# Backward scan outputs in token order, one set of turning products instead of two

## The chip, the cores and the metric

The kernel runs on one core of a Trainium2 chip. The metric is the device time of one execution in microseconds (us). In the text PE is TensorE (matrix products), DVE is VectorE, ACT is ScalarE, POOL is GpSimd and SP is SyncE, whose queue issues most DMAs. "L1300" is line 1300 of the kernel as it stands in the profile before.

## The reference, cut to what matters

One layer of a hybrid backbone runs over 640 tokens (512 latent, 128 context): a normalisation, a projection `w_in`, then 16 heads of a two-directional delta-rule scan beside a chunked gMLP, a projection `w_out`, and a SwiGLU mixer. The part that the change touches is the end of the scan:

```python
for d in range(2):                       # 0: forward, 1: backward
    ...
    y, s_fin = _delta_scan(rh, decay, kd, vh, -kk, kk * heads(a), s0[:, d], reverse=(d == 1))
    out = out + _group_norm(y, lp['gn_w'], lp['gn_b']) \
        + jnp.sum(rh * kd * lp['r_k'], axis=-1, keepdims=True) * vh
o = out.reshape(B, T, D_A) * gate
```

So the scan outputs `y` of both directions are normalised for each token and head, and summed for each token.

## The kernel before

All matrices with channels on partitions are 128 channels by 640 tokens. A "pair" p (0 to 7) is two heads, 128 channels. The scan is done in chunks of 64 tokens, ten chunks (eight of latent tokens, two of context).

**First stage** (to about 1085 us). For each pair and direction d, `rows` builds the tile `R`: for each chunk a half `R[:, :, 0, :]` made of the removal keys and a half `R[:, :, 1, :]` made of the queries `zr`. The function `rev` turns the tokens of each chunk round for d = 1, so that in the backward direction both halves lie in the order of the scan. `chunks` multiplies `X` (keys) with `R`, which gives for each chunk a 128 x 128 block; its right half, query against key, is masked (a query sees keys up to itself) into the tile `GR` and stored in DRAM with other pieces as the record of the chunk, `d_S`.

**Scan stage** (about 1085 to 1368 us). Time advances in "hops". `recur(p)` is a generator that takes three hops for each of eight steps; a new pair starts every 13 hops (`OFF`), and takes 26, so two pairs run side by side. In a step, the state products `w_ps` (L1193) are added on DVE to the tile `W` (L1202), which `u_ps` (L1213) multiplies; its result is copied into the record `rec` by DVE (L1217) and then ACT (L1218); `s_ps` (L1240) makes the new state from the record, and DVE turns it into `SN` (L1248) with the help of `SG` (L1224). `y_ps` (L1166, L1176) makes the outputs of the 64 tokens, which ACT copies into `u.Y[:, d, chunk, :]` (L1181), tokens on partitions (heads on two halves of them).

When a pair's scan has ended, `norm(p)` runs over the next hops: POOL subtracts the mean from `u.Y` (L1277), ACT squares, DVE sums, POOL takes the power -0.5 (L143) and multiplies (L1287). Two hops later `join(p, 0)` and one hop after it `join(p, 1)` turn five chunks each back to channels: in `join` (L1300), each product takes a 64 x 64 block of `u.Y` as weights and streams a 64 x 64 matrix past it, `I2` (the unit matrix) for d = 0 and `J2` (the unit matrix with its columns reversed) for d = 1. Both products add up in the same place of PSUM, so the sum over directions and the turn round of d = 1 are done by PE. DVE then joins the bonus term (L1303, `bv`). In the two hops after that `gate(p, hf)` makes four products `pmm` (L1312), and DVE multiplies `bv` by them (L1313).

Between these pieces PE is filled with products of `w_out` from the job list `m3` (L1081 to L1083, `big`), and with transposes of the input (L1338, `pxT`). The left operand of these is loaded by SP (`o_load`, L1067, `ol<-d_o`), rounded by ACT (L1068, `oh`) and split on DVE (L1069, `ol`).

What sets the order: on PE the scan stage is written out by hand (`manual_schedule`), so PE executes it in the order in which the code emits it. On the other engines, and in SP's queue, a scheduler orders the instructions by its own estimate of times; each engine then executes strictly in that order.

Of the kernel before, what the change touches and what calls it, by code (L numbers as in the profile page):

```python
# [10 lines left out]
F32 = mybir.dt.float32  # L11
# [3 lines left out]
ALU = mybir.AluOpType  # L15
# [4 lines left out]
P = 128  # L20
# [5 lines left out]
CH = 64  # L26
# [63 lines left out]
def flow_step(ctx: ExitStack, tc, x_prompt, x_sample, state_rwkv, c, c_ctx, w_mod, b_mod,  # L90
# [4 lines left out]
    V, S, G, TE = nc.vector, nc.scalar, nc.gpsimd, nc.tensor  # L95
# [21 lines left out]
    cb = cbx.enter_context(tpool(name="constb", bufs=1))  # L117
# [4 lines left out]
    I2 = cb.tile([P, CH], F32, name="I2")  # L122
    for h in range(2):
        s = slice(CH * h, CH * h + CH)
        V.tensor_copy(I2[s, :], ident[s, s])
    J2 = cb.tile([P, CH], F32, name="J2")
    V.tensor_copy(J2, I2[:, ::-1])
    mask = cb.tile([P, P], F32, name="mask")
    ones16 = cb.tile([P, CH], BF16, name="ones16")
    V.memset(ones16, 1.0)  # L130
# [237 lines left out]
    v3 = lambda ap: ap.rearrange("p (c t) -> p c t", t=CH)  # L368
# [195 lines left out]
    def take_k(pr, p):  # L564
        o = pairs[p]
        o.GB, o.dd = {}, {}
        zr, zv = o.zr, o.zv
# [63 lines left out]
        def rows(d, inner):  # L631

            rev = (lambda ap: ap[:, :, ::-1]) if d else (lambda ap: ap)
            tha, g3, i3 = thas[d], v3(gams[d]), v3(Ls[d])
            Rs[d] = R = bz.tile([P, NCH, 2, CH], F32, tag="R", name="R")
            ra = rev(R[:, :, 0, :])
            if d:
                V.tensor_mul(ra[:, :, 0:CH - 1], n3[:, :, 0:CH - 1], g3[:, :, 1:CH])
                S.copy(ra[:, :, CH - 1], n3[:, :, CH - 1])
            else:  # L640
                V.tensor_mul(ra[:, :, 1:CH], n3[:, :, 1:CH], g3[:, :, 0:CH - 1])
                S.copy(ra[:, :, 0], n3[:, :, 0])
            yield 0.8
            V.tensor_mul(rev(R[:, :, 1, :]), v3(zr), g3)
            yield 0.8
            nc.sync.dma_start(d_S[p, :, d, :, F_R:F_R + P], R.rearrange("p c s t -> p c (s t)"))
            Zs[d] = Z = bz.tile([P, NCH, 2, CH], F32, tag="Z", name="Z")
            vsrc = d_vt[p, d].rearrange("(c t) v -> t c v", t=CH)
            for h in range(2):
                nc.sync.dma_start(Z[hsl(h), :, h, :], vsrc[:, :, hsl(h)])  # L650
            f = fs if d == 0 else bk.tile([P, T], F32, tag="t1", name="f", bufs=2)
            V.tensor_scalar(f, tha, kah[:, p:p + 1], ka1[:, p:p + 1], op0=ALU.mult, op1=ALU.add)
            V.tensor_mul(f, f, zk)
            yield 1.2
            V.scalar_tensor_tensor(out=tha, in0=tha, scalar=1.0, in1=nkk, op0=ALU.add, op1=ALU.mult)
            yield 0.8

            for e in ((0, 1), (1, 0)):
                V.scalar_tensor_tensor(out=rev(X[hsl(e[0]), :, e[1], :]), in0=v3(tha)[hsl(e[0])], scalar=-0.5,
                                       in1=i3[hsl(e[0])], op0=ALU.mult, op1=ALU.mult)  # L660
            yield 1.5
            if d == 1:
                V.tensor_add(fs, fs, f)
            yield from inner
            V.tensor_mul(rev(X[0:64, :, 0, :]), v3(f)[0:64], i3[0:64])
            V.tensor_mul(rev(X[64:128, :, 1, :]), v3(f)[64:128], i3[64:128])
            yield 1.5

        def chunks(d):

            R, Z = Rs[d], Zs[d]
            n = 2 * p + d
            mixM.until(lambda: len(merged) > n - 4)
            o.GB[d] = GB = bp.tile([P, NCH, CH], F32, tag=f"GB{n % 4}", name="GB")

            GA = bk.tile([P, NCH, CH], F32, tag="GA", name="GA")
            for (c0, c1) in ((0, 4), (4, 8), (8, NCH)):
                two = [ps.rearrange("p (c t) -> p c t", t=P) for ps in both("pG")]
                in_turn([lambda cc=cc, h=h: TE.matmul(
                    two[h][:, cc - c0, :], X[hsl(h), cc].rearrange("p s t -> p (s t)"),  # L680
                    R[hsl(h), cc].rearrange("p s t -> p (s t)"), start=True, stop=True)
                    for cc in range(c0, c1) for h in range(2)])
                S.copy(GB[osl(0), c0:c1, :], two[0][osl(0), 0:c1 - c0, 0:CH])
                for h in (1, 0):
                    s, q, ps = hsl(h), osl(h), two[h]
                    mb = mask.unsqueeze(1).to_broadcast([P, c1 - c0, P])
                    GR = bk.tile([P, 4, CH], F32, tag="GR", name="GR", bufs=2)
                    V.tensor_tensor(out=GR[:, 0:c1 - c0, :], in0=ps[:, 0:c1 - c0, CH:P], in1=mb[:, :, CH:P], op=ALU.mult)
                    V.tensor_tensor(out=GA[s, c0:c1, :], in0=ps[s, 0:c1 - c0, 0:CH], in1=mb[s, :, 0:CH], op=ALU.mult)
                    if h:  # L690
                        S.copy(GB[q, c0:c1, :], ps[q, 0:c1 - c0, 0:CH])
                    nc.sync.dma_start(d_S[p, :, d, c0:c1, F_G + CH * h:F_G + CH * h + CH], GR[:, 0:c1 - c0, :])
                yield 0.5 * (c1 - c0)

            for (c0, c1) in ((0, 8), (8, NCH)):
                two = [ps.rearrange("p (c t) -> p c t", t=CH) for ps in both("pXT")]
                in_turn([lambda cc=cc, h=h: TE.transpose(
                    two[h][:, cc - c0, :], X[hsl(h), cc].rearrange("p s t -> p (s t)"), ident[hsl(h), hsl(h)])
                    for cc in range(c0, c1) for h in range(2)])
                for h in range(2):  # L700
                    ps = two[h]
                    XT = bz.tile([P, 8, CH], F32, tag="XT", name="XT", bufs=2)
                    S.copy(XT[:, 0:c1 - c0, :], ps[:, 0:c1 - c0, :])
                    nc.sync.dma_start(d_S[p, :, d, c0:c1, F_X + CH * h:F_X + CH * h + CH], XT[:, 0:c1 - c0, :])
                yield 0.2 * (c1 - c0)
            two = [ps.rearrange("p (c t) -> p c t", t=CH) for ps in both("pW0")]
            for c0 in (0, 5):
                ps = two[c0 // 5][:, 0:5, :]
                for cc in range(c0, c0 + 5):
                    for h in range(2):  # L710
                        TE.matmul(ps[osl(h), cc - c0, :], GA[hsl(h), cc, :], Z[hsl(h), cc, h, :], start=True, stop=True)
                for h in range(2):
                    S.copy(Z[osl(h), c0:c0 + 5, h, :], ps[osl(h)])
                yield 1.0
            nc.sync.dma_start(d_S[p, :, d, :, F_Z:F_Z + P], Z.rearrange("p c h v -> p c (h v)"))
            o.dd[d] = db.tile([8, NCH, 16, 16], F32, tag=f"dd{d}", name="dd")
            for gq in range(8):
                q = gq % 4
                BQ.dma_start(o.dd[d][gq].rearrange("c s t -> s c t"),
                             GB[16 * gq:16 * gq + 16, :, 16 * q:16 * q + 16])  # L720
# [376 lines left out]
    with ExitStack() as ph:  # L1097
# [160 lines left out]
        def norm(p):  # L1258
# [14 lines left out]
            for d in range(2):  # L1273
                y, ys = u.Y[:, d], u.ys[:, d]
                G.tensor_scalar(ys, ys, 1.0 / CH, None, op0=ALU.mult)
                for (a, b) in HV:
                    G.tensor_tensor(out=y[:, a:b], in0=y[:, a:b], in1=bc(ys[:, a:b], b - a), op=ALU.subtract)  # L1277
                yield
                sq = rw.tile([P, NCH, CH], F32, tag="sq", name="sq")
                for (a, b) in HV:  # L1280
                    S.activation(sq[:, a:b], y[:, a:b], AF.Square)
                    V.tensor_reduce(out=ys[:, a:b], in_=sq[:, a:b], axis=AX.X, op=ALU.add)
                yield
                G.tensor_scalar(ys, ys, 1.0 / CH, GN_EPS, op0=ALU.mult, op1=ALU.add)
                rsqrt(ys, ys)
                for (a, b) in HV:
                    G.tensor_tensor(out=y[:, a:b], in0=y[:, a:b], in1=bc(ys[:, a:b], b - a), op=ALU.mult)  # L1287
                yield

        HV = ((0, 5), (5, NCH))  # L1290

        def join(p, i):

            u = U[p]
            a, b = HV[i]
            ps = po.tile([P, 5, CH], F32, tag="g", name="pO")
            for cc in range(a, b):
                for h in range(2):
                    for d in range(2):
                        TE.matmul(ps[hsl(h), cc - a, :], u.Y[hsl(h), d, cc, :], (J2 if d else I2)[hsl(h), :],  # L1300
                                  start=(d == 0), stop=(d == 1))
            dst = v3(u.bv)[:, a:b, :]
            V.scalar_tensor_tensor(out=dst, in0=ps, scalar=prm[:, C_GW + p:C_GW + p + 1],  # L1303
                                   in1=dst, op0=ALU.mult, op1=ALU.add)
# [866 lines left out]
```

## Time and profile before

| | |
|---|---|
| median of 3 runs | 3190.33 us (3187.9 to 3195.78) |
| the profiled execution | 3191.31 us, of which its span is 3189.5 us |
| granted PE clock | 0.991 |
| PE busy | 3075.3 us, 96% of the span |
| DVE busy | 2347.6 us, 74% |
| ACT busy | 1474.9 us, 46% |
| POOL busy | 1220.2 us, 38% |

The profiled execution is 1.0 us above the median. "Busy" of PE counts a product until its modelled end, so short products that are issued one behind the other overlap in it.

### The profile page before, as it was taken

The numbers are of one execution on the slowest core, as the hardware profiler recorded it, in microseconds if no ns is written. First come the engines' busy times: TensorE is split into PE (matmuls) and PEld (weight loads), VectorE is DVE, ScalarE is ACT, GpSimd is POOL, SyncE is SP. The second block draws the span as 40 slices with busy tenths as digits, with TensorE's granted clock in tenths as the row PEclk, the third lists the DMA queues.
The fourth block names the chain that finished last, engine by engine and source line by source line (L and its number), as shares of the span: only waits on it lengthen the run. The fifth ranks groups of instructions, "written<-read, shape, count | busy, mean of one in ns | idle before, by whom it ended". The sixth has DMA issues, their size and how long they took to land.

```text
span 3189.5 us, 72242 instructions
## 1 busy us (share of the span) xinstructions
PE 3075.3 (96%) x28216; PEld 2861.3 (90%) x28216; DVE 2347.6 (74%) x4120; ACT 1474.9 (46%) x3216; POOL 1220.2 (38%) x1065
## 2 busy tenths in 40 slices
PE   6899999999999999999999999999999999999997
PEld 4688878788878888899999999999999999999997
DVE  4566777667775678767877878777777788877788
ACT  3344544454444444346544444444444445444365
POOL 2001121221122024411465666656655655555542
PEclk9999999999999999999999999999999999999999
DMA  9767786777777688475344434443344365553453
GB/s 370 245 192 202 217 231 172 212 199 212 221 202 193 214 275 268 153 210 162 97 125 128 122 107 127 119 121 119 109 130 126 108 194 156 163 160 119 143 165 123
DMA packets 740439, 550.89 MB, mean 173 GB/s; under 512 B 141056, under 2 KB 673504, under 8 KB 731264
## 3 DMA queue, kind: packets, MB, share of 16 engines
q1 hardware_dynamic: 727136, 532.47, 55.3%
q0 software_dynamic: 10624, 13.23, 1.8%
q8 instruction: 222, 3.64, 0.5%
q14 instruction: 121, 0.99, 0.1%
q10 hardware_dynamic: 2336, 0.57, 0.1%
HBM read 437.79 MB, written 110.95 MB: 172 GB/s over the span
## 4 chain that ended last, share of the span: by engine, by line
PE 73%; DVE 10%; issue 6%; DMA 6%; ACT 3%; POOL 2%; SPq 0%; DVEq 0%; POOLq 0%; ACTq 0%
PE P L1688 15%; PE P L1685 15%; PE P L1686 15%; PE big L196 5%; PE big L200 4%; PE big L197 4%; DMA raw<-in_w_in_dram 1%; PE pm L948 1%; DVE lo L1466 1%; PE big L1081 1%; PE big L1524 1%; PE big L1525 1%; PE big L1526 1%; PE big L1082 1%; PE big L1083 1%
## 5 line engine op out<-in xcount | busy, mean ns | idle before, releaser
L1685 PE MATMUL P<-xo,hi 128*128 128x320 f32 x2352 | 700.5, 310 | 0.2 <-ACT hi L1465 0.2
L1686 PE MATMUL P<-xo,hi 128*128 128x320 f32 x2352 | 700.4, 309 | 0.0
L1466 DVE TENSOR_TENSOR lo<-raw,hi 128x512 fp32r<-128x512 f32 x526 | 517.8, 989 | 161.6 <-ACT hi L1465 158.7
L1465 ACT CAST hi<-raw 128x512 fp32r<-128x512 f32 x526 | 326.7, 622 | 468.4 <-PE P L1686 397.6
L1688 PE MATMUL P<-xo,lo 128*128 128x320 f32 x2352 | 441.8, 310 | 4.1 <-DVE lo L1466 4.1
L196 PE MATMUL big<-h_hi,hi 128*128 128x320 f32 x1376 | 438.2, 325 | 7.8 <-ACT hi L174 4.4
L1685 PEld LDWEIGHTS P<-xo,hi 128*128 128x128 f32 x2352 | 442.3, 188 | 0.5 <-ACT hi L1465 0.5
L1686 PEld LDWEIGHTS P<-xo,hi 128*128 128x128 f32 x2352 | 442.7, 188 | 0.0
L197 PE MATMUL big<-h_lo,hi 128*128 128x320 f32 x1376 | 422.6, 314 | 0.8 <-DVE h_lo L360 0.8
L1594 POOL TENSOR_TENSOR raw<-raw 128x512 f32<-128x512 f32 x252 | 410.5, 1638 | 10.1 <-DVE lo L1466 1.8
L1688 PEld LDWEIGHTS P<-xo,lo 128*128 128x128 f32 x2352 | 370.0, 188 | 4.9 <-DVE lo L1466 4.9
L1685 PE MATMUL P<-xd,hi 128*128 128x320 f32 x1232 | 367.8, 310 | 6.1 <-ACT P L2079 2.8
L1686 PE MATMUL P<-xd,hi 128*128 128x320 f32 x1232 | 366.8, 309 | 0.0
L200 PE MATMUL big<-h_hi,lo 128*128 128x320 f32 x1376 | 319.8, 312 | 3.9 <-DVE lo L175 2.1
L196 PEld LDWEIGHTS big<-h_hi,hi 128*128 128x128 f32 x1376 | 261.8, 190 | 58.2 <-issue 26.1
L175 DVE TENSOR_TENSOR lo<-raw,hi 128x512 fp32r<-128x512 f32 x268 | 185.4, 695 | 157.6 <-ACT hi L174 153.9
L1594 POOL TENSOR_TENSOR t<-raw 128x512 f32<-128x512 f32 x84 | 123.7, 1472 | 427.5 <-DMA raw<-in_w_ffn_up_dram 415.9
L1465 ACT CAST hi<-rawd 128x512 fp32r<-128x512 f32 (+1 forms) x288 | 167.1, 586 | 225.3 <-PE P L1686 148.9
L174 ACT CAST hi<-raw 128x512 fp32r<-128x512 f32 x268 | 164.4, 617 | 225.9 <-PE big L197 84.9
L197 PEld LDWEIGHTS big<-h_lo,hi 128*128 128x128 f32 x1376 | 261.6, 190 | 5.8 <-DVE h_lo L360 1.9
L1466 DVE TENSOR_TENSOR lo<-rawd,hi 128x512 fp32r<-128x512 f32 (+1 forms) x288 | 231.9, 812 | 24.9 <-ACT hi L1465 24.2
L1688 PE MATMUL P<-xd,lo 128*128 128x320 f32 x1232 | 236.6, 310 | 4.2 <-DVE lo L1466 4.2
(408 smaller groups left out, 6129.7 us busy)
## 6 DMA issues: line engine op xcount, KB each, us to landing
wt<-in_w_mod_dram SPq DMA_DIRECT2D x96, 1024.0 KB
raw<-in_w_ffn_gate_dram SPq DMA_DIRECT2D x182, 256.0 KB
raw<-in_w_ffn_up_dram SPq DMA_DIRECT2D x182, 256.0 KB
rec<-d_S SPq DMA_DIRECT2D x80, 576.0 KB
raw<-in_w_in_dram SPq DMA_DIRECT2D x172, 256.0 KB
rawd<-in_w_ffn_down_dram SPq DMA_DIRECT2D x128, 256.0 KB
raw<-in_w_out_dram SPq DMA_DIRECT2D x96, 256.0 KB
xd<-d_os SPq DMA_DIRECT2D x66, 320.0 KB
```

Of the source, the lines that this page charges most:

```text
L174: S.copy(hi, raw)
L175: V.tensor_sub(lo, raw, hi.bitcast(F32))
L196: TE.matmul(halves[hf], hi[:, k, :], h_hi[:, kb, s], start=(kb == 0), stop=False)
L197: TE.matmul(halves[hf], hi[:, k, :], h_lo[:, kb, s], start=False, stop=False)
L200: TE.matmul(halves[hf], lo[:, j - 4 * q, :], h_hi[:, j, s], start=False, stop=(j == KB - 1))
L948: TE.matmul(pm[32 * j:32 * j + 2, :], cT[:, 2 * (kb + u):2 * (kb + u) + 2], quad[:, u, j, :], start=(kb + u == 0), stop=(kb + u == KB - 1) ...
L1465: S.copy(hi[:, 0:nk], raw[:, 0:nk])
L1466: V.tensor_sub(lo[:, 0:nk], raw[:, 0:nk], hi[:, 0:nk].bitcast(F32))
L1594: G.tensor_tensor(out=o[:, 0:nk], in0=p[:, 0:nk], in1=q[:, 0:nk], op=ALU.subtract)
L1685: TE.matmul(ps, hi[:, k, :], xk[:, 0, :], start=q == 0 and k == 0 and not filled, stop=False)
L1686: TE.matmul(ps, hi[:, k, :], xk[:, 1, :], start=False, stop=False)
L1688: TE.matmul(ps, lo[:, k, :], x(i, 4 * q + k)[:, 0, :], start=False, stop=q == nq - 1 and k == nk - 1 and last)
```

## The change

The queries of the backward direction are stored in the natural order of tokens instead of the order of the scan. The order of queries in `R` is the order of the scan's output rows, so the outputs of d = 1 come out in natural order too, and the mask of their scores is read with its columns reversed. In `norm`, after the multiplication for d = 1, POOL adds the normalised outputs of d = 0 to those of d = 1 (two instructions for each pair, 16 in all). `join` then needs the product with `I2` alone, ten products instead of twenty; `J2` and the copy that made it fall away.

```diff
-    J2 = cb.tile([P, CH], F32, name="J2")
-    V.tensor_copy(J2, I2[:, ::-1])
...
-            V.tensor_mul(rev(R[:, :, 1, :]), v3(zr), g3)
+            V.tensor_mul(R[:, :, 1, :], v3(zr), g3)
...
                     mb = mask.unsqueeze(1).to_broadcast([P, c1 - c0, P])
+                    mr = mask[:, CH:P][:, ::-1] if d else mask[:, CH:P]
+                    mr = mr.unsqueeze(1).to_broadcast([P, c1 - c0, CH])
                     GR = bk.tile([P, 4, CH], F32, tag="GR", name="GR", bufs=2)
-                    V.tensor_tensor(out=GR[:, 0:c1 - c0, :], in0=ps[:, 0:c1 - c0, CH:P], in1=mb[:, :, CH:P], op=ALU.mult)
+                    V.tensor_tensor(out=GR[:, 0:c1 - c0, :], in0=ps[:, 0:c1 - c0, CH:P], in1=mr, op=ALU.mult)
...
                     G.tensor_tensor(out=y[:, a:b], in0=y[:, a:b], in1=bc(ys[:, a:b], b - a), op=ALU.mult)
+                    if d:
+                        G.tensor_tensor(out=y[:, a:b], in0=y[:, a:b], in1=u.Y[:, 0, a:b], op=ALU.add)
...
             for cc in range(a, b):
                 for h in range(2):
-                    for d in range(2):
-                        TE.matmul(ps[hsl(h), cc - a, :], u.Y[hsl(h), d, cc, :], (J2 if d else I2)[hsl(h), :],
-                                  start=(d == 0), stop=(d == 1))
+                    TE.matmul(ps[hsl(h), cc - a, :], u.Y[hsl(h), 1, cc, :], I2[hsl(h), :], start=True, stop=True)
```

On PE the first join stands between `u_ps` and `s_ps` of a step. Before (the products with `I` and `J` alternate, twenty in all; the first four are shown):

```order
L1213 MATMUL u_ps<-W,rec 64x64 x4
L1300 MATMUL pO<-I_68,Y 64x64
L1300 MATMUL pO<-J_71,Y 64x64
L1300 MATMUL pO<-I_68,Y 64x64
L1300 MATMUL pO<-J_71,Y 64x64
```

And with the change, at the same place:

```order
L1213 MATMUL u_ps<-W,rec 64x64 x4
L1301 MATMUL pO<-I_68,Y 64x64 x10
L1240 MATMUL s_ps<-rec 64x64 x4
L1081 MATMUL big<-oh,hi 128x320
L1082 MATMUL big<-ol,hi 128x320
L1083 MATMUL big<-oh,lo 128x320
```

Nothing else moves on PE: each of the 16 joins has ten products fewer at its place.

On the engines that the scheduler orders, some instructions of the scan stage stand elsewhere. On DVE, at the gate of pair 0 (`bv<-bv,gb,pmm` is L1313, `ol` the split of a `w_out` operand), before:

```order
L1202 TENSOR_TENSOR W<-w_ps,rec 64x128 x2
L1069 TENSOR_TENSOR ol<-ol,oh 128x640
L1313 SCALAR_TENSOR_TENSOR bv<-bv,gb_1111,pmm 128x320
L1217 COPY rec<-u_ps 64x2x64
L1313 SCALAR_TENSOR_TENSOR bv<-bv,gb_1111,pmm 128x320
L1069 TENSOR_TENSOR ol<-ol,oh 128x640
```

And with the change:

```order
L1202 TENSOR_TENSOR W<-w_ps,rec 64x128 x2
L1313 SCALAR_TENSOR_TENSOR bv<-bv,gb_1109,pmm 128x320
L1217 COPY rec<-u_ps 64x2x64
L1313 SCALAR_TENSOR_TENSOR bv<-bv,gb_1109,pmm 128x320
L1269 TENSOR_TENSOR gate<-graw,gate 128x128
L1271 TENSOR_TENSOR gate<-graw,gate 64x128
L1069 TENSOR_TENSOR ol<-ol,oh 128x640
```

The split no longer stands ahead of the two multiplications of the gate. At the gate of pair 2 the same happens with the first of the two multiplications; there the split now stands just ahead of the second.

On ACT, two of the four casts `oh<-ol` of that group of operands move behind later work. Before, some 15 us after that gate (`Y` are copies of outputs, `rec` the copies of the step, `hi` a cast of weights):

```order
L1181 ACTIVATE Y,ys<-y_ps 128x64 x4
L1218 COPY rec<-u_ps 64x2x64
L174 CAST hi<-raw 128x512
L1218 COPY rec<-u_ps 64x2x64
L1181 ACTIVATE Y,ys<-y_ps 128x64 x2
```

And with the change:

```order
L1181 ACTIVATE Y,ys<-y_ps 128x64 x4
L1068 CAST oh<-ol 128x640
L1218 COPY rec<-u_ps 64x2x64
L172 CAST hi<-raw 128x512
L1068 CAST oh<-ol 128x640
L1218 COPY rec<-u_ps 64x2x64
```

The two casts now stand each ahead of a `rec` copy. In SP's queue the loads that they wait for moved back too: they stand behind three loads of records and all loads of `graw`, where before they stood ahead of these.

## The prediction

> **What bounds the kernel now.** I read the page first, then the scan stage alone, since only there instructions are removed and added: busy time by stretches, PE's waits, the joins in the timeline.
>
> ```profile
> PE 3075.3 (96%) x28216; PEld 2861.3 (90%) x28216; DVE 2347.6 (74%) x4120; ACT 1474.9 (46%) x3216; POOL 1220.2 (38%) x1065
> ```
>
> PE is the bound over the whole program. The stretches of the scan stage (PE, weight loads, DVE, ACT, POOL, clock, DMA share, GB/s):
>
> ```profile
> 1085.00:1160.00 75.00, 74.61 (x1256) 62.89 (x1255) 52.71 (x182) 30.99 (x146) 10.68 (x14) 1.00 0.90 273
> 1160.00:1235.00 75.00, 70.45 (x1261) 59.48 (x1260) 59.33 (x188) 35.51 (x159) 27.94 (x38) 0.98 0.82 262
> 1235.00:1310.00 75.00, 73.54 (x1402) 62.90 (x1401) 59.37 (x196) 28.58 (x148) 26.16 (x33) 1.00 0.82 261
> 1310.00:1368.00 58.00, 55.45 (x661) 50.06 (x662) 35.56 (x92) 15.99 (x59) 22.49 (x28) 1.00 0.25 76
> ```
>
> PE is busy for 274.05 of 283 us here too, so work taken from PE has a good chance to shorten the stage. What PE waits for in this stage (who, for whom, us in total, times, longest):
>
> ```profile
> PE w_ps L1193 <- DVE SN L1248: 2.0, 4, 0.7
> PE pmm L1312 <- DVE bv L1313: 2.0, 2, 1.1
> PE big L1081 <- DVE x1T L1094: 1.5, 1, 1.5
> PE s_ps L1240 <- ACT rec L1218: 1.3, 3, 0.7
> PE u_ps L1213 <- DVE W L1202: 0.9, 2, 0.7
> PE pxT L1338 <- DVE bv L1313: 0.6, 1, 0.6
> PE pxT L1338 <- DVE bv L1303: 0.3, 1, 0.3
> ```
>
> 8.6 us in all, none of it for a DMA or for POOL: DMA engines are busy at 0.82 to 0.90, but their data come early enough for PE.
>
> **The products removed.** By form, both kinds of product of the joins:
>
> ```profile
> L1300 PE MATMUL pO<-I,Y 64*64 64x64 f32 x320 | 20.4, 221 | 0.0
> L1300 PE MATMUL pO<-J,Y 64*64 64x64 f32 x320 | 20.2, 218 | 0.0
> ```
>
> Each product has two records, so 160 of each kind. The 218 ns are from issue to result, and the busy times of the two rows overlap; neither is the price. The price is the pace in the timeline, here pair 0's first join:
>
> ```profile
> 1151.61 0.45 PE L1213 MATMUL u_ps<-W,rec 64*64 64x64 f32 x8
> 1151.90 0.33 PE L1300 MATMUL pO<-I,Y 64*64 64x64 f32 x4
> 1152.01 0.33 PE L1300 MATMUL pO<-J,Y 64*64 64x64 f32 x4
> ...
> 1152.95 0.33 PE L1300 MATMUL pO<-J,Y 64*64 64x64 f32 x4
> 1153.21 0.45 PE L1240 MATMUL s_ps<-rec 128*64 128x64 f32 x8
> ```
>
> Ten groups of two products (four records) start from 1151.90 to 1152.95: nine steps of 0.117 us, so a product costs 0.0585 us. The join takes 10 x 0.117 = 1.17 us plus the switch to the next shape. Ten products fewer are 0.585 us for each join, and 16 x 0.585 = 9.4 us for all. The eight records of `u_ps` above, four products, take 0.29 us until the join starts (0.07 us each with their start), and these go to the two halves of the array in turn, as the products of the changed join do; so the pace should stay.
>
> **What comes back at once.** The first join stands between `u_ps` and `s_ps`, and hides the copies of `u_ps` into the record:
>
> ```profile
> 1152.42 0.26 ACT L1218 COPY rec<-u_ps 64x128 f32<-64x128 f32 x1 [0.41 <-DVE rec L1217]
> ```
>
> That copy ends at 1152.68, and `s_ps` started at 1153.21, 0.53 us later. A join that is 0.585 us shorter asks for `s_ps` at 1152.62, just before the copy is done; with some 0.04 us from the copy's end to the product, 0.1 us comes back. Pairs 0 to 5 have this form, so 6 x 0.1 = 0.6 us. With the last two pairs no second scan runs beside, and for the second joins nothing like it follows at once: their `s_ps` uses a record made long before. Bounds: nothing, and 8 x 0.585 = 4.7 us if each first join only turns into waiting.
>
> **The additions on POOL.** 16 instructions of 128x320 with two full inputs. No such addition is in the stage; the nearest rows:
>
> ```profile
> L1277 POOL TENSOR_TENSOR Y<-Y,ys 128x320 f32<-128x320 f32 x32 | 24.0, 769 | 1.3
> L1287 POOL TENSOR_TENSOR Y<-Y,ys 128x320 f32<-128x320 f32 x32 | 23.3, 748 | 1.3
> L1494 POOL TENSOR_TENSOR sumq<-sumq,sq 128x320 f32<-128x320 f32 x14 | 15.6, 1113 | 38.6 <-issue 21.8 <-ACT sq L1488 16.8
> ```
>
> The last is the same instruction elsewhere, so I take 1.1 us (between 0.75 and 1.1): 2.2 us for each pair at the end of `norm`. POOL is busy for 87 of 283 us, so what matters is only whether a join has to wait. Tightest is pair 6:
>
> ```profile
> 1327.20 1.50 POOL L1287 TENSOR_TENSOR Y<-Y,ys 128x320 f32<-128x320 f32 x2
> 1329.89 0.34 PE L1300 MATMUL pO<-I,Y 64*64 64x64 f32 x4
> ```
>
> The multiplications end at 1328.70, the addition of the first five chunks at some 1329.8: the join is just served (if it waited for both additions, 1.0 us). The other pairs have several us. So 0, and up to 1.0.
>
> The other price is DVE. Its `SG` reads two SBUF inputs:
>
> ```profile
> L1224 DVE TENSOR_TENSOR SG<-SN,gend x64: 273/278/819, 1092.0 to 1332.3; 128x128 f32<-128x128 f32 x64
> L1224 DVE TENSOR_TENSOR SG<-SN,gend 128x128 f32<-128x128 f32 x64 | 22.4, 357 | 0.6
>   PEld w_ps L1193: 1.0, 5
>   PEld u_ps L1213: 0.9, 5
> ```
>
> Median 278 ns, mean 357, longest 819: 64 x 0.079 = 5.1 us lost, which I lay to the 47.3 us of POOL's passes over `Y`. The waits for `SG` that end at PE's weight loads are 1.9 us. New POOL work of 16 x 1.1 = 17.8 us costs in proportion 1.9 us of DVE, and PE 1.9 x 17.8 / 47.3 = 0.7 us. Bounds: 0, and the longest delay, 0.54 us, 16 times, 8.7 us. The Trainium skill ("SBUF — State Buffer", Who interferes with whom) says that a VectorE instruction with two SBUF inputs and a GpSimd instruction that reads SBUF contend for one read interface, and that the loser is blocked for the whole instruction. The trace agrees in kind (273 to 819 ns); by the rule at its worst, each addition blocking for its 1.1 us, the sum would be 17.8 us instead of 0.7.
>
> **The instructions that the scheduler moved.** At the gate of pair 0, and again at that of pair 2:
>
> ```profile
> 1153.63 0.50 SPq L1067 DMA_DIRECT2D ol<-d_o  x1
> 1159.86 0.73 ACT L1068 CAST oh<-ol 128x640 fp32r<-128x640 f32 x1 [1.20 <-DMA ol<-d_o]
> 1160.62 0.82 DVE L1069 TENSOR_TENSOR ol<-ol,oh 128x640 fp32r<-128x640 f32 x1 [0.79 <-ACT oh L1068]
> 1161.96 0.85 PE L1312 MATMUL pmm<-gss,gate 128*128 128x320 f32 x4 [0.89 <-DVE bv L1313]
> 1225.75 0.85 PE L1312 MATMUL pmm<-gss,gate 128*128 128x320 f32 x4 [1.07 <-DVE bv L1313]
> ```
>
> A load took 6.2 us to land, ACT waited for it, DVE for ACT, the gate's multiplication for DVE, and PE 0.89 us for that. With the split behind the gate, both waits can go, at most 1.96 us; I take 1.6, since PE still waits for its own first `pmm` to be multiplied. Against it, two casts now stand ahead of `rec` copies on ACT, and their loads are issued later. If a load lands late, the copy waits, behind it `s_ps`. Between nothing and the 6.2 us of a whole landing; I take 1.3 us, a wait like that at 1159.86. Net -0.3 us, with bounds of -2.0 and +6.2.
>
> **At nothing.** `R` with queries in natural order, and the mask read backwards:
>
> ```profile
> L644 DVE TENSOR_TENSOR R<-zr,gam x16: 803/817/821, 206.4 to 932.2; 128x640 f32<-128x640 f32 x16
> L688 DVE TENSOR_TENSOR GR<-pG,mask x96: 216/418/426, 213.9 to 963.1; 128x256 f32<-128x256 f32 x64, 128x128 f32<-128x128 f32 x32
> ```
>
> L644 writes eight times forward and eight times backward, 803 to 821 ns: the direction costs nothing. A mask read backwards has no row; were it twice as slow, 48 x 0.42 = 20 us of DVE would be spread over 750 us beside a busier PE (over the program DVE is busy for 74%, PE for 96%). `J2`'s copy is a single DVE instruction during the first loads.
>
> **The sum.** -9.4 + 0.6 + 0.7 - 0.3 = -8.4 us: 3191.3 - 8.4 = 3182.9 against the profiled execution, which is 1.0 us above the median of the runs; against the median, 3182.
>
> **Rivals.**
> - More than the sum. The waits at the gates of pairs 0 and 2 go, and the moved casts find their data landed: -9.4 + 0.6 + 0.7 - 1.9 = -10.0, so 3180.3. For it: the 0.89 and 1.07 us have the split right ahead of them. Against it: the loads behind the moved casts are issued later. 0.27.
> - Given back in the scan's own chain. ACT stands at a moved cast for most of a landing, or the shorter first joins leave `s_ps` and then `w_ps` waiting: +5 us on the sum of the other terms (-9.4 + 0.6 + 0.7), so 3186.6. For it: `w_ps` already waits for `SN` four times. Against it: PE's waits are only 8.6 us of the stage. 0.20.
> - Slower than before. Each addition holds DVE's second read for its whole 1.1 us, always while `SG` or a split is due: -9.4 + 0.6 + 17.8 = +9.0, so 3199. It decides from 0.55 us for each addition. Against it: `SG` lost 5.1 us under 64 such passes, 0.08 each. This is the page's rule named above, at its worst. 0.03.
> - No effect, because products with `J` ran in the shadow of those with `I`: 3190. For it: records of both kinds overlap. Against it: starts follow each other in steps of 0.117 us without a hole. 0.03.
>
> **How the numbers follow.** The sum's own case has 0.47. Range: down to 3176 (-9.4 and -2.0, without any return, is 3179 on the median, and 3 us for the spread of medians), up to 3188.5 (the second rival's 3186.6 and the same spread on a smaller part); what is left out are the last two rivals and the tails. A measurement tells about 0.3% from no change, 9.6 us, so faster means below 3180.8: from the sum's own case, 3182 with some 3 us either way, four in ten (0.18), and of the first rival two in three (0.18): 0.36. Slower, 0.03. The rest, 0.61, is the same.
>
> **What would show it.** Joins of 0.6 us instead of 1.2 (five groups at 0.117); `s_ps` after a first join with a short wait for the copy of `rec`; POOL's additions near 1.1 us, at the end of each `norm`, and joins that don't wait for POOL; `SG` with a mean a little above 357; PE's waits for `bv` at the first gate gone; the scan stage some 8 us shorter, the stages before and after as long as they were. It would be wrong if ACT stands at `oh` for several us, or if `w_ps` and `s_ps` wait more by what the joins lost.

## The result, and the profile after

The changed kernel takes 3182.17 us (median of 10 runs, 3177.96 to 3185.68) against 3190.68 of the kernel before beside it: a ratio of 0.9968, 95% interval 0.9955 to 0.998. Timed once more beside other kernels it was 0.9975 (0.9964 to 0.9985), 3182.95 against 3192.72. So it is faster by 0.2% to 0.45%; the medians stand 8.5 and 9.8 us apart. Forecast were 3182 and a sum of -8.4 us. In the second set the mean granted clock was 0.9911, in the kernel before 0.9903: of its 9.8 us at most some 2.5 can be clock.

The profiled execution takes 3182.42 us, its span 3180.6, at a granted clock of 0.993. The page's first part, and the four stretches of the scan stage (PE, weight loads, DVE, ACT, POOL, clock, DMA share, GB/s):

```profile
PE 3059.6 (96%) x27896; PEld 2844.7 (89%) x27896; DVE 2354.6 (74%) x4119; ACT 1474.4 (46%) x3216; POOL 1238.2 (39%) x1081
```

```profile
1085.00:1160.00 75.00, 74.00 (x1193) 62.38 (x1192) 54.82 (x182) 31.21 (x147) 12.42 (x16) 1.00 0.87 266
1160.00:1235.00 75.00, 70.68 (x1271) 59.32 (x1270) 62.95 (x199) 36.28 (x165) 34.62 (x44) 1.00 0.87 282
1235.00:1310.00 75.00, 73.54 (x1316) 62.40 (x1316) 61.66 (x202) 30.27 (x155) 30.46 (x37) 1.00 0.80 254
1310.00:1368.00 58.00, 55.47 (x557) 50.92 (x554) 38.07 (x92) 20.33 (x58) 25.82 (x32) 1.00 0.40 118
```

320 records of products are gone (28216 to 27896), 16 instructions of POOL have come. PE is about as full as before in each stretch; the stage just ends sooner. From the first `w_ps` to the last `pmm` it takes 268.2 us instead of 278.9; the stage ahead ends 2.0 us later (1089.2 against 1087.2), and what follows takes 1823.2 us against 1823.5: the span's -8.9 us is the scan stage's -10.7 and that spread. Of the -10.7, 1.4 us aren't the change but a halved clock in the profile before (shown below); that leaves -9.3. A join in the timeline, and the group of all joins:

```profile
1154.50 0.45 PE L1213 MATMUL u_ps<-W,rec 64*64 64x64 f32 x8
1154.78 0.75 PE L1301 MATMUL pO<-I,Y 64*64 64x64 f32 x20
1155.31 0.26 ACT L1218 COPY rec<-u_ps 64x128 f32<-64x128 f32 x1 [0.41 <-DVE rec L1217]
1155.46 0.45 PE L1240 MATMUL s_ps<-rec 128*64 128x64 f32 x8
```

```profile
L1301 PE MATMUL pO<-I,Y 64*64 64x64 f32 x320 | 12.2, 219 | 0.0
```

From the join's first product to the next tile's are 0.68 us, where before there were 1.31 (1151.90 to 1153.21). PE's waits in the stage (who, for whom, us, times, longest):

```profile
PE w_ps L1193 <- DVE SN L1248: 2.5, 5, 0.9
PE s_ps L1240 <- ACT rec L1218: 2.1, 4, 0.9
PE u_ps L1213 <- DVE W L1202: 1.6, 3, 1.1
PE big L1081 <- DVE x1T L1094: 1.5, 1, 1.5
PE pxT L1338 <- DVE bv L1313: 0.6, 1, 0.6
PE pxT L1338 <- DVE bv L1303: 0.3, 1, 0.3
PE pmm L1312 <- DVE bv L1313: 0.3, 1, 0.3
```

8.9 us, before 8.6: the waits at the gates (`pmm`, 2.0 before) are down to 0.3, and the scan's own chain (`w_ps`, `s_ps`, `u_ps`) has 6.2 where it had 4.2.

**The stage cut into stretches.** The medians of two kernels tell 8 us from nothing, but not 1 us. The traces tell more. PE's order in the stage is the same in nearly all kernels here, but for the products in the joins, so the stage can be cut at the `swap` products, two for each pair. Five of the 16 stretches (three ahead of the first join, one behind pair 1's joins, one behind pair 4's) agree to some 0.03 us in the traces of the table. The rest is added up in three groups: A with the joins of pairs 0 and 1, B with those of pairs 2 to 4, C with those of pairs 5 to 7. "Stage" goes from the start of the first `w_ps` to the start of the last `pmm`; "cast" is how long ACT waited, at pair 2's gate, for the load of the `w_out` operand that its cast `oh` reads; "half clock" is how many us of the stage, and of which group, were granted half the clock of PE.

| kernel | products in a join | additions | stage, us | A | B | C | cast | half clock |
|---|---|---|---|---|---|---|---|---|
| before | 20 | - | 278.9 | 61.54 | 86.13 | 78.21 | 0.60 | 3.4 (A) |
| natural_only | 20 | - | 278.4 | 59.81 | 87.36 | 78.24 | 0.81 | 0 |
| add_only | 20 | 16 | 279.7 | 61.53 | 86.91 | 78.21 | 0.78 | 0 |
| short_p0 | 20, pair 0: 10 | 16 | 280.8 | 59.50 | 90.06 | 78.24 | 1.03 | 10.1 (B) |
| products_only | 10 | - | 267.9 | 57.88 | 82.56 | 74.42 | 0.43 | 0 |
| no_add | 10 | - | 267.4 | 57.38 | 82.57 | 74.41 | 0.36 | 0 |
| after | 10 | 16 | 268.2 | 58.21 | 82.58 | 74.41 | 0.54 | 0 |
| after_again | 10 | 16 | 273.2 | 58.98 | 86.80 | 74.41 | 2.39 | 3.4 (B) |
| add_x4 | 10 | 64 | 271.6 | 58.76 | 85.43 | 74.42 | 0.28 | 3.4 (B) |
| long_p0 | 10, pair 0: 20 | 16 | 274.4 | 60.47 | 86.44 | 74.42 | 2.46 | 6.7 (B) |

C shows the price of the products without anything else: six joins, 3.80 us, 0.633 us each in every pair of kernels. B shows what a single profile can't: the same kernel (after and after_again) differs by 4.2 us there.

Part of such differences is PE's clock. These are the stretches of half clock in before, after_again, add_x4, long_p0 and short_p0, in this order (columns as above, the clock ahead of the DMA share):

```profile
1164.00:1167.40 3.40, 3.40 (x38) 2.83 (x37) 1.61 (x6) 0.43 (x4) 0.17 (x1) 0.50 0.60 198
1257.80:1261.20 3.40, 3.40 (x36) 2.83 (x36) 1.78 (x8) 0.52 (x2) 3.15 (x5) 0.50 0.59 186
1262.40:1265.80 3.40, 3.40 (x38) 2.84 (x40) 1.85 (x8) 0.52 (x2) 3.15 (x5) 0.50 0.56 178
1230.30:1237.00 6.70, 6.47 (x79) 5.25 (x78) 4.88 (x18) 2.30 (x11) 5.21 (x8) 0.50 0.74 254
1227.90:1238.00 10.10, 9.71 (x133) 8.04 (x127) 6.81 (x24) 4.12 (x19) 8.66 (x12) 0.50 0.65 204
```

In after_again the 3.4 us fall into pair 4's joins, whose stretch takes 28.34 us there and 26.94 in the changed kernel's first profile, with the same waits of PE: 1.4 us. In before the same steps take 1.4 us longer than in natural_only, which has its full clock in the stage. What halves the clock in one execution and not in another isn't shown.

### The profile page after: what moved, and what is told of

It is laid out like the page before. It is cut to its first block, busy times and chain, and to the rows that moved or that the text cites. A ratio compares the mean times of both kernels' runs of the same rounds, so it can differ in the third digit from the quotient of the medians.

```text
span 3180.6 us, 71623 instructions
## 1 busy us (share of the span) xinstructions
PE 3059.6 (96%) x27896; PEld 2844.7 (89%) x27896; DVE 2354.6 (74%) x4119; ACT 1474.4 (46%) x3216; POOL 1238.2 (39%) x1081
## 4 chain that ended last, share of the span: by engine, by line
PE 45%; DVE 3%; issue 1%; DMA 1%; POOL 1%; ACT 0%; SPq 0%; DVEq 0%; POOLq 0%; ACTq 0%
PE P L1688 15%; PE P L1685 15%; PE P L1686 15%; DVE lo L1466 1%; DMA opd<-d_op 0%; DVE xd L1754 0%; DMA x1d<-d_x 0%; POOL rawd L1594 0%; DVE cd L1944 0%; DMA rawd<-in_w_ffn_down_dram 0%; DVE out L2138 0%; DVE acc L1925 0%; ACT hi L1465 0%; DMA xd<-d_os 0%; POOL t L1594 0%
## 5 line engine op out<-in xcount | busy, mean ns | idle before, releaser
L1594 POOL TENSOR_TENSOR raw<-raw 128x512 f32<-128x512 f32 x252 | 410.2, 1637 | 10.1 <-DVE lo L1466 1.8
L1466 DVE TENSOR_TENSOR lo<-rawd,hi 128x512 fp32r<-128x512 f32 (+1 forms) x288 | 241.3, 844 | 24.6 <-ACT hi L1465 24.3
```

Source lines behind the costliest of these rows:

```text
L1466: V.tensor_sub(lo[:, 0:nk], raw[:, 0:nk], hi[:, 0:nk].bitcast(F32))
L1594: G.tensor_tensor(out=o[:, 0:nk], in0=p[:, 0:nk], in1=q[:, 0:nk], op=ALU.subtract)
```

## Experiments: the two parts of the change

**products_only**, the kernel before without the products for d = 0:

```diff
-                    for d in range(2):
-                        TE.matmul(ps[hsl(h), cc - a, :], u.Y[hsl(h), d, cc, :], (J2 if d else I2)[hsl(h), :],
-                                  start=(d == 0), stop=(d == 1))
+                    TE.matmul(ps[hsl(h), cc - a, :], u.Y[hsl(h), 1, cc, :], J2[hsl(h), :], start=True, stop=True)
```

> The kernel before, with the join's products for d = 0 left out (ten products with the reversed matrix instead of twenty; no additions, old order of queries; the outputs of the forward direction are missing from the result). DVE, ACT and SP execute in the order of the changed kernel. Theory (the sum of the prediction without the additions: -9.4 + 0.6 - 0.3 = -9.1): 3181.6 us against 3190.7 before. Rival 1, the chain gives back more than it shows and only the additions or the order of queries hide it: 3186 or more. Rival 2, products in the shadow of each other: 3190. If the additions of the changed kernel cost as much as 4 us, this kernel is at 3178.

3183.03 against 3192.82 us, ratio 0.9969 (0.9957 to 0.998); stage 267.9 us. The products alone give what the whole change gives. Both rivals (chain, shadow) fall.

**no_add**, the changed kernel without the two POOL lines in `norm`:

> The changed kernel without POOL's 16 additions (the forward direction's outputs are missing from the result); everything else in the order of the changed kernel. Theory (additions slow DVE's SG in proportion, 0.7 us of PE): 3181.5 us, and SG's mean back from 374 to some 357 ns. Rival 1, the additions cost nothing: 3182.2. Rival 2, each addition holds DVE for its whole length (16 x 0.95 = 15 us): 3167. With products_only it must agree within 0.1% if the natural order of queries is free.

0.9974 (0.9962 to 0.9986): the totals can't tell it from the changed kernel. The stage can: 267.4 against 268.2 us. All of the 0.8 us is in A. Its main part repeats: the stretch with pair 0's joins takes 27.48 us in both kernels with ten products there and no additions (products_only, no_add), and 28.35 or 28.36 in all seven with ten products there and additions on POOL. The place is pair 0's end. The changed kernel, then the kernel without additions, at the same steps of the program:

```profile
1146.83 1.19 DVE L1224 TENSOR_TENSOR SG<-SN,gend 128x128 f32<-128x128 f32 x2
1146.95 1.79 POOL L1289 TENSOR_TENSOR Y<-Y 128x320 f32<-128x320 f32 x2
1147.94 1.35 DVE L173 TENSOR_TENSOR lo<-raw,hi 128x512 fp32r<-128x512 f32 x1
...
1149.42 0.46 DVE L1248 SCALAR_TENSOR_TENSOR SN<-s_ps,gend,SG 128x64 f32<-128x64 f32 x2
...
1149.74 0.33 PE L1193 MATMUL w_ps<-SN,rec 64*64 64x64 f32 x4 [0.62 <-DVE SN L1248]
```

```profile
1144.64 0.52 DVE L1224 TENSOR_TENSOR SG<-SN,gend 128x128 f32<-128x128 f32 x2
1145.09 0.68 DVE L173 TENSOR_TENSOR lo<-raw,hi 128x512 fp32r<-128x512 f32 x1
...
1146.34 0.48 DVE L1248 SCALAR_TENSOR_TENSOR SN<-s_ps,gend,SG 128x64 f32<-128x64 f32 x2
...
1146.86 0.33 PE L1193 MATMUL w_ps<-SN,rec 64*64 64x64 f32 x4
```

Beside the two additions (1.79 us) the two `SG` take 1.19 instead of 0.52 us and a split of weights 1.35 instead of 0.68: DVE loses 1.34 us, `SN` comes late, and PE waits 0.62 us.

DVE isn't slowed here but held. The split that starts at 1147.94 ends at 1149.29; its usual 0.68 us reach back to 1148.61, 0.13 us before the second addition ends (1148.74). Every DVE instruction of the stage that lost more than 0.04 us beside an addition fits this, four in the changed kernel and 18 in add_x4: it ends its usual time after a point 0.12 to 0.13 us before the addition's end. And where DVE comes first, the addition waits. At pair 4 in the changed kernel, two `SG` and a split take their usual time, and the first of the two additions 1.81 us instead of some 0.9:

```profile
1264.81 0.48 DVE L1224 TENSOR_TENSOR SG<-SN,gend 128x128 f32<-128x128 f32 x2
1264.83 2.63 POOL L1289 TENSOR_TENSOR Y<-Y 128x320 f32<-128x320 f32 x2
1265.21 0.68 DVE L173 TENSOR_TENSOR lo<-raw,hi 128x512 fp32r<-128x512 f32 x1
```

**add_x4**, three more additions behind each:

```diff
+                    for _ in range(3 if d else 0):
+                        G.tensor_tensor(out=junk[:, a:b], in0=y[:, a:b], in1=u.Y[:, 0, a:b], op=ALU.add)
```

> The changed kernel with three more additions behind each of the 16, into a tile that nobody reads, behind what the joins wait for: 48 more instructions, some 46 us more of POOL. Theory (proportion, 1.9 us of PE for 47 us of such passes): +1.8 us, 3184. Rival 1, nothing: 3182.2. Rival 2, whole blocking whenever SG is due, at worst the 46 us: up to 3228; it has begun to be true above 3192. SG's mean by theory: +17 ns for each 15 us of additions, so 374 + 50 = 425 ns.

3185.34 us, 0.9978 (0.9967 to 0.9989); stage +3.4 us against one profile of the changed kernel (the forecast was +1.8; 3228, where all 46 us would have held DVE, is out: its 18 holds make 8.5 us). The cast at pair 2's gate waits only 0.28 us here, so the 2.85 us more in B aren't a late load as in after_again. They stand in pair 4's joins, and 1.4 of them are steps at half clock (1262.4 to 1265.8, above), not additions; without these the stage is 2.0 us longer, near the forecast. Behind them one sees what the additions do:

```profile
1269.61 1.30 DVE L1224 TENSOR_TENSOR SG<-SN,gend 128x128 f32<-128x128 f32 x2
...
1269.86 5.58 POOL L1291 TENSOR_TENSOR junk<-Y 128x320 f32<-128x320 f32 x6
1270.84 1.36 DVE L173 TENSOR_TENSOR lo<-raw,hi 128x512 fp32r<-128x512 f32 x1
...
1272.64 0.52 PE L1193 MATMUL w_ps<-SN,rec 64*64 64x64 f32 x7 [0.88 <-DVE SN L1248]
```

**add_only**, the changed kernel with twenty products in each join:

```diff
+                    for d in range(2):
+                        TE.matmul(ps[hsl(h), cc - a, :], u.Y[hsl(h), d, cc, :], I2[hsl(h), :],
+                                  start=(d == 0), stop=(d == 1))
```

> The changed kernel with the ten products of each join put back (a second product with the unit matrix and the tile of d = 0, so the forward outputs count twice in the result): twenty products, 16 additions, natural order. DVE, ACT and SP execute in the order of the kernel before. Theory (only the additions' price is left): 3190.7 + 0.7 = 3191.4 us. Rival, the additions hold DVE for their whole length: 3206. If it comes out at 3186 or less, the gain isn't from the products.

3195.4 against 3192.82, 1.0008 (0.9997 to 1.0019), stage 279.7 against 278.9. With the products back, the gain is gone. The stage's 0.8 us more isn't a second measurement of the additions: it stands in B, not in A, and before and natural_only, neither of which has additions, lie 1.7 us apart in A and 1.2 in B.

**natural_only**, the kernel before with `R` and the mask of the changed kernel and `I2` for both directions:

> The kernel before with the queries in natural order and the mask read backwards for d = 1, and the join's two products both with the unit matrix (twenty products, no additions); every engine executes in the order of the kernel before. Theory (natural order costs nothing): 3190.7 us, the first stage ending as early as before (first w_ps at 1087 us), the scan stage 278.9 us from the first w_ps to the last pmm. Rival, the mask read backwards is twice as slow on DVE and half of that reaches PE: 3200, GR rows of 418 and 836 ns.

3194.93 against 3194.33, 1.0002 (0.999 to 1.0013). The mask read backwards, to be compared with 216/418/426 before:

```profile
L690 DVE TENSOR_TENSOR GR<-pG,mask x96: 216/418/427, 214.3 to 968.9; 128x256 f32<-128x256 f32 x64, 128x128 f32<-128x128 f32 x32
```

It costs nothing. The first `w_ps` stood at 1093.7 us here and not at 1087; in the other kernels with the natural order it stands anywhere from 1084.5 (after_again) to 1092.2, so that is spread of the first stage.

**add_dve**, the additions on DVE (`V.tensor_add` in place of `G.tensor_tensor`):

> The changed kernel with the 16 additions on DVE instead of POOL. Nearest row for their length: the split of weights, 128x512 with two SBUF inputs, 676 ns, so 0.43 us each, 6.9 us of DVE; the 2.3 us that SG and the splits lose to POOL's additions come back. Theory (DVE time reaches PE by a third, as 2.3 us of DVE cost 0.8 us of the stage): scan stage 268.2 + 1.6 = 269.8 us, 3184 in all. Rival 1, DVE is on the scan's chain wherever the additions stand: 268.2 - 0.8 + 6.9 = 274.3, 3188. Rival 2, cheaper than POOL's: 267.4, 3181.

3222.94 us, 1.0083 (1.0068 to 1.0099), stage 307.3: all three expectations missed, by 35 us at the least. What DVE waited for, the additions by themselves, and PE's longest waits:

```profile
DVE Y L1289 <- POOL Y L1287: 23.2, 7, 5.2
```

```profile
L1289 DVE TENSOR_TENSOR Y<-Y x16: 477/480/994, 1146.1 to 1376.2; 128x320 f32<-128x320 f32 x16
```

```profile
PE w_ps L1193 <- DVE SN L1248: 17.4, 10, 3.8
PE big L1081 <- DVE x1T L1094: 6.7, 2, 5.3
PE s_ps L1240 <- ACT rec L1218: 5.5, 4, 4.2
```

I had counted the additions' length (480 ns at the median, near the estimate of 0.43 us) and not what they wait for. Each needs the multiplication that POOL has just been given, DVE executes in order, and it stands 23.2 us at them. On POOL the trace has no idle time ahead of the additions: the producer is the instruction ahead.

The waits aren't all of the 39 us that the stage is longer than in the changed kernel. PE waits for 32.8 us in it instead of 8.9. Most of the rest is clock (the stage of the changed kernel, then this one, clock 1.00 and 0.94):

```profile
1089.20:1357.40 268.20, 258.88 (x4225) 220.41 (x4225) 206.16 (x651) 109.35 (x507) 103.33 (x128) 1.00 0.74 235
1089.00:1396.30 307.30, 274.06 (x4226) 233.26 (x4226) 212.91 (x667) 109.55 (x507) 87.32 (x112) 0.94 0.66 205
```

Some 34 us of the stage were at half clock, and PE's steps in them take 12.6 us longer than the same steps of the changed kernel. All five executions had a clock of 0.984 to 0.986, the kernel before beside them 0.987 to 0.993. Six of the seven waits of PE over 2.5 us have half clock starting within 3 us of their end; but before and after_again have it without such a wait, so that the waits bring it on is likely and not shown.

## Experiments: the moved casts

**long_p0** and **short_p0**, the changed kernel with twenty products in some pairs only (`n` is 2 for pair 0 and 1 elsewhere, and the reverse):

```diff
+                    n = 2 if p == 0 else 1
+                    for d in range(n):
+                        TE.matmul(ps[hsl(h), cc - a, :], u.Y[hsl(h), 1 - d, cc, :], I2[hsl(h), :], start=(d == 0), stop=(d == n - 1))
```

> The changed kernel with twenty products in the two joins of pair 0 only (the second ten with the unit matrix and the forward tile, so these outputs count twice). The casts oh, the splits ol and their loads at the gate of pair 0 stand again as in the kernel before. Stage from the first w_ps to the last pmm, 268.2 us in the changed kernel: the two joins give back 1.25. If the moved instructions are worth 1.0 to 1.5 us in the stage, as the balance of the other kernels says (278.9 - 10.0 for the joins = 268.9, but 267.4 and 267.9 without additions), 270.5 to 271; if they are worth nothing, as -0.3 + 0.6 of the prediction says within 0.3, 269.5.

> The reverse: twenty products in all joins but the two of pair 0, with 16 additions. The casts and loads at the gate of pair 0 stand as in the changed kernel, those of pair 2 as before. Stage by the joins and the additions alone: 279.7 (the twenty products with additions) - 1.25 = 278.4 us. If the instructions moved at pair 0's gate are worth 1.0 to 1.5 us: 277.0 to 277.5.

274.4 and 280.8 us in one execution each (3193.03 and 3203.16 us in all): above both expectations, and in the wrong place. A, where pair 0's instructions moved, has 60.47 and 59.50; with the joins and the additions taken out (0.633 and 0.83 us), and 1.4 us for before's half clock, A has 57.9 us as the mean of the four kernels with the order of before at pair 0 (57.3 to 58.4), and 57.65 of the five with the moved order (57.4 to 58.15). So the move is worth about 0.2 us, less than its own scatter. What spoiled both totals lies in B: in short_p0 the 10.1 us of half clock, whose steps take 3.1 us longer than in add_only; in long_p0 6.7 us of it in pair 3's joins (27.04 us instead of 25.28) and a late load at pair 2's gate, as in the next experiment.

**after_again**, the changed kernel itself:

> The changed kernel itself, for how well one profile repeats: stage from the first w_ps to the last pmm 268.2 us within 0.5 us (the two kernels with the order before stand 0.45 us apart), the end of the stage before it anywhere from 1087 to 1094 us; 3182 us, 0.997 of before.

The total repeats (0.9975), the stage doesn't: 273.2. Pair 2's gate in the changed kernel's first profile, then in this one:

```profile
1222.66 0.73 ACT L1068 CAST oh<-ol 128x640 fp32r<-128x640 f32 x1 [0.54 <-DMA ol<-d_o]
...
1223.41 0.26 ACT L1218 COPY rec<-u_ps 64x128 f32<-64x128 f32 x1
1224.66 0.40 PE L1240 MATMUL s_ps<-rec 128*64 128x64 f32 x8
1225.45 0.52 PE L1193 MATMUL w_ps<-SN,rec 64*64 64x64 f32 x7 [0.39 <-DVE SN L1248]
```

```profile
1221.65 0.72 ACT L1068 CAST oh<-ol 128x640 fp32r<-128x640 f32 x1 [2.39 <-DMA ol<-d_o]
1222.40 0.26 ACT L1218 COPY rec<-u_ps 64x128 f32<-64x128 f32 x1
1222.72 0.45 PE L1240 MATMUL s_ps<-rec 128*64 128x64 f32 x8 [0.75 <-ACT rec L1218]
1224.34 0.52 PE L1193 MATMUL w_ps<-SN,rec 64*64 64x64 f32 x7 [1.17 <-DVE SN L1248]
```

The same load was issued 4.9 us (1217.75) and 7.8 us (1213.84) before its cast could start. ACT stands at the cast, behind it the copy of `rec`, then `s_ps`, `SN`, `w_ps`. Pair 2's joins and gate take 30.69 us instead of 27.90: 2.8 of B's 4.2 us. The other 1.4 are the half clock in pair 4's joins. This is the prediction's second rival, at a cast whose move I overlooked in the section on the change. In the kernel before, ACT had copies of `Y` behind the same cast, and idle time ahead of the copy of `rec`:

```profile
1223.65 0.73 ACT L1068 CAST oh<-ol 128x640 fp32r<-128x640 f32 x1 [0.60 <-DMA ol<-d_o]
1224.40 0.22 ACT L1181 ACTIVATE Y<-y_ps 128x64 f32<-128x64 f32 x1
...
1225.96 0.26 ACT L1218 COPY rec<-u_ps 64x128 f32<-64x128 f32 x1 [1.04 <-issue]
```

The same order stands in natural_only, add_only and short_p0; in these four the cast waited for 0.60 to 1.03 us. The other six of the table have the `rec` copy right behind the cast, and two of them, after_again and long_p0 (2.46 us), had a late load. That the load is late isn't shown to come from the change; that ACT's cushion behind the cast is gone does come from it.

**early_ol**: the second group's loads are issued behind the first's, and their casts go to the start of the stage.

```diff
-                    o_load(kb)
+                    if q == 0: o_load(kb)
+                    else: o_split(kb)                  # cast and split alone
                     yield 1.0
+                if q == 0:
+                    for kb in range(12, 16): o_load(kb)  # the load alone
```

> The changed kernel with the four loads ol of the second w_out group issued right behind those of the first group, at the start of the scan stage; the scheduler then puts their casts and splits there too, so none stands at the gate of pair 0. Theory (a cast that waits for its load holds the copy of rec behind it, and s_ps): the 1.1 us that PE waits for s_ps near 1182 us goes, and the stage from the first w_ps to the last pmm is 267.2 us against 268.2; in all 3181, not to be told from the changed kernel. Rival 1, the casts cost nothing where they stand: 268.2. Rival 2, the loads (1.3 MB, some 5 us at 270 GB/s) delay records at the start of the stage: 270 or more.

3185.41 us, 0.9978 (0.9967 to 0.999), stage 268.2. In the stretch with pair 1's joins the wait for `s_ps` goes (0.9 us in the trace, not the 1.1 of the expectation; 27.32 us against 27.90), but as much is spent near the stage's start, where the splits now stand. The first rival is nearest.

**late_ol4** and **late_ol5**: the loads of pairs 0 to 3 wait for pair 4's, or pair 5's, `bv`.

```diff
+            if kb < 4:
+                G.tensor_copy(o_lo[kb][:, 0:1], U[4].bv[:, T - 1:T])   # U[5] in late_ol5
             nc.sync.dma_start(raw, d_o[kb])
```

> The changed kernel with the loads ol of the first four scan pairs held back: one column of each is first written by POOL from pair 4's finished bv, so load, cast and split move from the gate of pair 2 and the stretch behind it to some 80 us later. PE's order is as in the changed kernel. Theory (one landing of such a load, 4.9 us in one execution and 7.8 in another, holds ACT at the cast, the copy of rec behind it, s_ps, and costs the stage up to 5 us): the stage from the first w_ps to the last pmm at 268.2 us or a little below, without the 3.7 us stretch at pair 2's gate; 3181 in all, 2 us below the changed kernel on average. Rival 1, the same wait comes back where the casts stand now: 268 to 273, 3183. Rival 2, POOL's column copies hold the norm behind them: over 273.

> The same, held back to pair 5's bv, so the four casts stand in the stretch where pair 7 scans alone. Theory: as late_ol4, 268.2 us, since PE waits there for the chain only where no w_out products are left. Rival 1, with one pair alone each delay of ACT goes straight to PE: four casts of 0.7 us, 271. In all 3181 by the theory, 3184 by the rival.

3184.23 us, 0.9974 (0.996 to 0.9987), and 3187.19 us, 0.9971 (0.9959 to 0.9984). The stage is 269.0 and 270.0 us. B is 82.7 in both, free of the late load, but C is 75.0 and 76.2 instead of 74.4: first rival. A new wait in late_ol4 shows why pair 6's join was priced at all:

```profile
PE pO L1303 <- POOL Y L1291: 1.1, 1, 1.1
```

No version is measurably faster than the changed kernel.

## Why the prediction was right, point by point

- **Products, -9.4.** Measured -10.1: 16 x 0.633. The pace of 0.0585 us for a product holds (`u_ps` to join to `s_ps` above). The term is 0.7 too small since I took ten steps between starts and left out the end: the last two records of a join start 0.054 us apart before, and 0.007 us in the changed kernel, where products go to the two halves in turn, so each join saves 0.05 us more at its end.
- **Given back at `s_ps`, +0.6.** It didn't happen: this step was misread. Behind the first join `s_ps` starts at 1155.46, while the copy of `rec` that I thought it needs runs from 1155.31 to 1155.57. In `recur` a pair's `u_ps` and `s_ps` are one hop apart; with pairs 13 hops apart, the `u_ps` ahead of the join and the `s_ps` behind it belong to different pairs. Nothing was hidden there.
- **Additions, +0.7.** 0.8 measured, close by luck: two errors cancel. `SG`'s mean rises from 358 to 374 ns, 1.0 us of DVE instead of 1.9; what I hadn't seen is that the splits `lo` and `ol`, also with two SBUF inputs, lose 1.3 us more (`lo` 680 to 705 ns, `ol` 814 to 891, in the stage). The additions took 948 ns in the mean, not 1.1 us. A price in proportion to POOL's time is an average over a few whole holds, and depends on which instructions meet.
- **The lock, 3199.** The time is refuted by add_x4, the lock isn't. The prediction's rule was that of the Trainium skill ("SBUF — State Buffer", Who interferes with whom). The traces agree with it: only DVE instructions with two SBUF inputs grow, the means of the other forms (`W`, `SN`, `bv`, `x1T`, the copies of `rec`) stay within 2 ns even in add_x4, and one that starts beside a running addition is held for what is left of it, all but 0.12 to 0.13 us. What the rival had wrong is how often: four of the 16 additions held DVE, for 2.5 us in all instead of 17.8, since only 5.8 of the additions' 15 us fell on such an instruction, and in part of that DVE came first.
- **Moved instructions, -0.3.** About -0.2 at pair 0's gate, within its scatter. Both halves of the term came: PE's wait for `bv` at the gates fell from 2.0 to 0.3 us, and a wait for `s_ps` behind a moved cast came (0.9 us at 1181.8). The prediction left out the cast that moved at pair 2's gate, where a late load costs 2.8 us.
- **Pair 6's join**, 0 of the 0 to 1.0: no wait in the changed kernel, 1.1 in late_ol4, where POOL is a little later.
- **Natural order at nothing**: right, within the 4 us that the totals can tell.
- **The rivals.** The stage (-9.3 without before's half clock) and the medians (-8.5 and -9.8) lie between the sum (-8.4) and the first rival (-10.0), and don't decide between them. The second exists as a mechanism (2.8 us at pair 2's gate in after_again), in some executions of the changed order and in none of the four profiles with the old one. Its 3186.6 is a slip: by its own terms it is 3190.3 - 8.1 + 5 = 3187.2.

Terms as measured: -10.1 + 0.8 - 0.2 = -9.5 us. The mechanism was right: the products are nearly the whole gain. The product term 0.7 too small and the return of 0.6 that doesn't exist don't cancel, both promised too little; the sum is 1.1 us off, which medians 1.3 us apart can't show. That the first median hit 3182 so closely was luck.

## What to carry to other kernels

Where one engine's order is fixed, cut two traces at the same instructions and compare the stretches: 0.6 us became visible that way, where medians scatter by several us, but profile the same kernel twice and read the granted clock of the stretch before it is believed: 3.4 us at half clock look like 1.4 us of cause. Work moved off the bounding engine costs what its new engine's queue holds up: on POOL, behind its own producer, 16 additions cost 0.8 us; on DVE the stage grew by 39, of which 24 are waits of PE and 12.6 steps at half clock. Before a wait is priced, make sure that the two instructions belong to the same chain.

## What the runs showed of the hardware that was not expected

- A VectorE instruction with two SBUF inputs that starts beside a running GpSimd addition is held until 0.12 to 0.13 us before its end and then takes its usual time (a split 1.35 us in all instead of 0.68). A GpSimd addition that comes behind such VectorE instructions is held in turn (1806 ns, the median is 890).
- Products of 64x64 that go to the two halves of the array in turn start their records in steps of 0.007 and 0.052 us; with two in a row in the same half the steps are 0.054 and 0.004. The pace of 0.0585 us for each product is the same.
- One and the same 128x640 load was ready for use 4.9 us after its issue in one execution and 7.8 in another.
- The granted clock of PE falls to a half for 3.4 to 10.1 us in the scan stage of some executions and not of others, at different places; 3.4 us of it cost 1.4 us.
